# Chunked recurrence of an encoder block: order of the in-chunk products and place of the output products

## The chip, the cores and the metric

The kernel runs on one core of a Trainium2 chip. The metric is the device time of one execution in microseconds (us); lower is better. The engines are TensorE (PE, with its weight loads shown apart as PEld), VectorE (DVE), ScalarE (ACT), GpSimd (POOL) and SyncE (SP, which only issues transfers here).

## What is computed

One layer of a hybrid encoder on 256 tokens of width 2048, float32 in and out. The part that the change touches is the RWKV-7 time mixing: 16 heads of 64 features, scanned forward and backward. Cut to what matters:

```python
def wkv7_scan(r, w, k, v, kk, a, reverse):
    def step(state, inp):
        r_t, w_t, k_t, v_t, kk_t, a_t = inp
        sa = einsum('bhvk,bhk->bhv', state, kk_t)
        state = (state * w_t[:, :, None, :] - sa[..., None] * (kk_t * a_t)[:, :, None, :]
                 + v_t[..., None] * k_t[:, :, None, :])
        return state, einsum('bhvk,bhk->bhv', state, r_t)
    return lax.scan(step, zeros, xs, reverse=reverse)

o = head_group_norm(o_f + o_b, gn_g, gn_b)        # forward scan + backward scan
x = x + (sigmoid(gate_A) * (yA @ W_pA) + sigmoid(gate_B) * (yB @ W_pB)) @ W_out
x = x + ConvGLU(RMSNorm(x));  output = RMSNorm(x)
```

The large products around it (the input projection, the two branch projections, `W_out`, the three ConvGLU matrices) make up most of the arithmetic.

## The kernel before

All large products are one stream of weight chunks (`push`, `advance`, L191 to L249). A chunk is four blocks of 128x128 weights: SyncE loads it, ScalarE rounds it to a high part (L223), DVE makes the low part (L224), and PE runs per block one 512-wide matmul (L242, the high part against both parts of the activations) and one 256-wide matmul (L246, the low part). Splitting runs three chunks ahead of PE (`HL_AHEAD`).

The recurrence works on eight pairs of heads, the two heads of a pair on partitions 0 to 63 and 64 to 127 (index `hh`, "half"). A direction's 256 tokens are four chunks of 64 (`NC`, `C`). For each pair there are generators, which issue some instructions and then yield a pause: `rwkv_rates`, `rwkv_operands`, `rwkv_inverse`, `rwkv_chain`, `rwkv_norm`. `run` spreads a budget of weight chunks over these pauses, in proportion to their lengths, so that PE has weight-stream work while the other engines do the small steps. The loop over p sets the chain of pair p beside the inverse of pair p+1 (`abreast`: one step of each, then the inverse's pause), with the rates of pair p+2 at their side; then come the norm of pair p and the operands of pair p+2. The framework that compiles the program may still reorder instructions on an engine where it expects an operand to be late.

- `rwkv_inverse`: for each direction and each half, four products (L667), one per chunk, each with 64 rows by 128 columns, go into one PSUM bank of `ps_g` (two buffers); DVE multiplies the bank by a mask into `Gs` (L669). Then `keys_by_token` transposes keys through the same pool (L678), and six steps of 32x32 products (L704, L714, L725, twice) and two last ones (L744, L755) invert the triangles.
- `rwkv_chain`: for each of four steps i, products for Z (L783 or L786, 128x64 pieces of the array), a copy by ScalarE (L789), products for U (L795, 64x64 pieces), copies into `UV` (L799), products for the state S (L805, 128x64 pieces), and DVE's update of `ZR` (L814, L816). Pauses are `CY` long. After the four steps come the output products of all chunks: `UV` against `Gs` (L824, 128x64 pieces) and `ZR` against `AR` (L830, 64x64 pieces), which add up in one bank, chunks 0 and 1 ahead of a pause and 2 and 3 behind it. ScalarE copies the bank to `O` (L835). The chain has 13 pauses, the inverse 13.
- `rwkv_norm`: splits `O` (L173, L174) and sums over each head's features on PE (L540).

PSUM has eight banks: `ps_mm` 2, `ps_ms` 1, `ps_g` 2, `ps_t` 1, `ps_c` 2 (the chain's Z, U, S and outputs).

Of the kernel before, what the change touches and what calls it, by code (L numbers as in the profile page):

```python
# [17 lines left out]
P = 128  # L18
T = 256
# [12 lines left out]
# how the product stream is spread: weight chunks beside the gating unit, fill jobs beside each phase of the  # L32
# recurrence (LAST chunks stay for its end), and the weights of the phases' pauses
# [6 lines left out]
CHAIN_Y = 13 * CY  # L40
# [16 lines left out]
# per-feature vectors, one column per 128 features  # L57
# [12 lines left out]
# masks and identities, which depend on shapes alone  # L70
# [46 lines left out]
def hybrid_kernel(ctx: ExitStack, tc: tile.TileContext, xT, w_in, w_pa, w_pb, w_out, w_g, w_u, w_d,  # L117
# [24 lines left out]
    # derived columns  # L142
# [12 lines left out]
    # the first activation loads ACT's table beside the first loads  # L155
# [6 lines left out]
    def rsqrt(y, s, t):  # L162
        """y = s ** -0.5 elementwise (s, y, t: SBUF float32, distinct): a guess from the bits, two Newton steps."""
        V.tensor_scalar(out=y.bitcast(I32), in0=s.bitcast(I32), scalar1=-0.5, scalar2=RSQRT_MAGIC,
                        op0=ALU.mult, op1=ALU.add)
        for p1, p0 in ((-0.703952253, 0.703952253 * 2.38924456), (-0.5, 1.5 + 3.2e-7)):
            V.tensor_tensor(out=t, in0=y, in1=y, op=ALU.mult)
            V.scalar_tensor_tensor(out=t, in0=t, scalar=p1, in1=s, op0=ALU.mult, op1=ALU.mult)
            V.scalar_tensor_tensor(out=y, in0=t, scalar=p0, in1=y, op0=ALU.add, op1=ALU.mult)

    def split(dst, src):
        """dst[:, 0] + dst[:, 1] == src, each half exact in float32r."""
        A.copy(dst[:, 0], src)  # L173
        V.tensor_tensor(out=dst[:, 1], in0=src, in1=dst[:, 0].bitcast(F32), op=ALU.subtract)  # L174
# [10 lines left out]
    def push(wd, nk, act, done, wide=True):  # L185
        """queue one block of 128 features; done(PSUM tile): its halves sum to the product (wide: the high
        part of the weights passes once over [x_hi | x_lo]), or it is the product itself"""
        job = dict(wd=wd, nk=nk, act=act, done=done, wide=wide, ps=None, last=0)
        for k0 in range(0, nk, RK):
            n = min(RK, nk - k0)  # L190
            raws.append([job, k0, n, None])  # L191
            for s0 in range(0, n, HK):
                chunks.append([job, len(raws) - 1, s0, min(HK, n - s0), None])
        job["last"] = len(chunks)
        jobs.append(job)
        return job

    def pair_up(n):
        """the first two jobs of n raw loads each side by side: two products for each part of x that comes in"""
        order = [i + o for i in range(n) for o in (0, n)]  # L200
        at = {ri: i for i, ri in enumerate(order)}
        raws[:2 * n] = [raws[ri] for ri in order]
        first = sorted((c for c in chunks if c[1] < 2 * n), key=lambda c: at[c[1]])
        for i, c in enumerate(first):
            c[1] = at[c[1]]
            c[0]["last"] = i + 1
        chunks[:len(first)] = first
# [67 lines left out]
    # padded token buffers for the shift  # L275
# [5 lines left out]
    def feat(ft, outv, then=lambda: None):  # L281
        """token-shifted feature tile ft into outv ([P, T] or [P, 2, 128] view)."""
        return push(w_in[ft], KT, hact, lambda ps: shift(ft, ps, outv, then))
# [27 lines left out]
    def run(gens, budget, serial=False):  # L311
        """trace generators side by side (or one after the other), each (gen, sum of its pauses), with
        budget chunks of the product stream spread over their pauses"""
# [32 lines left out]
    # what waits for norm1 while the first products run  # L346
# [23 lines left out]
    # inner features of the decay and the rates, by direction: high and low parts, each on both partition halves  # L370
# [3 lines left out]
    # inner features of the gate: two parts of the first 128, and high, low, high parts of the last 32  # L374
# [79 lines left out]
    def abreast(*gens):  # L454
        """one step of each at a time; the pauses are those of the last"""
        live = list(gens)
        while live:
            step = 0
            for g in list(live):
                try:  # L460
                    step = next(g)
                except StopIteration:
                    live.remove(g)
            yield step
# [37 lines left out]
    # the mean's sum is done; u comes in beside the norm of v  # L502
# [9 lines left out]
    ps_c = es_r.enter_context(tc.tile_pool(name="ps_c", bufs=2, space=PSUM))  # L512
# [23 lines left out]
    def head_sums(b):  # L536
        """sums over each head's features"""
        ps = ps_ms.tile([P, 512], F32, name="ms", tag="ms")
        for o in range(2):
            PE.matmul(ps[:, 0:T], bones, b[:, o], start=(o == 0), stop=(o == 1))  # L540
        return ps[:, 0:T]


    def rwkv_rates(p):
        """decay and in-context rates, keys"""
        k, v3, r, _ = feats[p]
        # the matrices come on both partition halves; the upper half turns into the rounding errors of the lower
# [34 lines left out]
        # kk = normalised k * k_k  # L582
# [13 lines left out]
        # twice the direction's key  # L596
# [7 lines left out]
    def rwkv_operands(p):  # L604
        """the chunks' operands: decayed keys and queries, values by token"""
# [17 lines left out]
        # V with tokens on partitions, chunk pairs in both orders  # L623
# [6 lines left out]
        # [U | V] and [S | V] stacked on partitions, by step and direction  # L630
# [23 lines left out]
    def rwkv_inverse(p):  # L654
        """in-chunk products and the inverses of their triangles"""
# [3 lines left out]
        # in-chunk products: [beta | kappa]^T [alpha | rho | I]  # L659
        Gs = []  # L660
        for d in range(2):
            Gd = rt("Gs", [2, NC, 3, C], 4)
            for hh in range(2):
                rows = slice(C * hh, C * hh + C)
                gp = ps_g.tile([P, 512], F32, name="gp", tag="gp")
                for c in range(NC):
                    PE.matmul(gp[:, c * P:(c + 1) * P], BK[rows, d, c, hh:hh + 2, :].rearrange("p a b -> p (a b)"),  # L667
                              AR[rows, d, c].rearrange("p a b -> p (a b)"), start=True, stop=True)
                V.tensor_tensor(out=Gd[:, hh, :, 0:2, :].rearrange("p c a b -> p c (a b)"),  # L669
                                in0=gp.rearrange("p (c k) -> p c k", k=P),  # L670
                                in1=gmask[:, d, hh, None, :].to_broadcast([P, NC, P]), op=ALU.mult)
                yield GY
# [11 lines left out]
        # inverse of the unit triangular matrices I - A, A transposed being what Gs holds: exact on diagonal blocks of 2,  # L684
        # then of 8 and of 32. With Q the transposed inverse of the blocks so far and F = Q A' (A' the part of A^T that
        # the larger blocks add, F^4 = 0), the next Q is (I + F^2)(I + F) Q.
# [46 lines left out]
        # last doubling: the off-diagonal 32 x 32 block; Qf holds minus the transposed inverse  # L733
# [27 lines left out]
        # alpha in place of the used triangle: stacked operand of Z  # L761
# [8 lines left out]
    def rwkv_chain(p):  # L770
# [3 lines left out]
        # chunk recurrence, both directions side by side  # L774
        for i in range(NC):
# [21 lines left out]
            for hh in range(2):  # L797
                rows = slice(C * hh, C * hh + C)
                A.copy(UV[rows, i, :, hh, :], uc[rows, 0, :, 0:C])  # L799
            yield CY  # L800
            if i < NC - 1:
# [15 lines left out]
                yield CY  # L817
        # outputs of both directions
        oc = ps_c.tile([P, 512], F32, name="cc", tag="cc")
        for c in range(NC):  # L820
            st = (c, NC - 1 - c)
            for hh in range(2):
                for d in range(2):
                    PE.matmul(oc[C * hh:C * hh + C, C * c:C * c + C], UV[:, st[d], d, hh, :], Gs[d][:, hh, c, 1, :],  # L824
                              start=(d == 0), stop=False, tile_position=(0, C * hh))
            for d in range(2):
                for hh in range(2):
                    if st[d] > 0:
                        rows = slice(C * hh, C * hh + C)
                        PE.matmul(oc[rows, C * c:C * c + C], ZR[rows, st[d], d, hh, :], AR[rows, d, c, 1, :],  # L830
                                  start=False, stop=(d == 1 or st[1] == 0), tile_position=(C * hh, C * hh))
            if c == 1:
# [6 lines left out]
    def rwkv_norm(p):  # L839
        BK, UV, ZR, bv, lg = heads.pop(p)  # L840
        O = outs.pop(p)
        # head norm, gate
# [26 lines left out]
    # products that run beside the recurrence; what they give waits in DRAM  # L869
# [64 lines left out]
    # from here on there is room for loads that run further ahead  # L934
# [28 lines left out]
    # the rest of the stream; what its products read and feed is made below  # L963
# [111 lines left out]
def _lay_out(inp):  # L1075
# [6 lines left out]
    def feat_tiles(a):  # L1082
        """[..., 3488] -> [..., NFEAT * 128] in tile order"""
# [52 lines left out]
```

## Time and profile before

| | |
|---|---|
| time, median of 3 runs | 1585.49 us (1584.33, 1585.49, 1600.15) |
| span of the profiled execution, first to last instruction | 1582.7 us |
| PE busy | 1553.3 us, 98% |
| PE weight loads busy | 1349.3 us, 85% |
| DVE busy | 1223.6 us, 77% |
| ACT busy | 922.4 us, 58% |
| moved by DMA | 273.72 MB, mean 173 GB/s |
| granted TensorE clock, mean | 0.995 of full speed |

The profile lists the span of one execution; no other time of that execution is given. Matmuls are pipelined and the trace models their ends, so the distance from one start to the next says more than a duration, and a busy PE need not be a PE at its peak. Idle time of an engine that doesn't bound the stage costs nothing.

### The profile page before, as it was taken

How to read it: one execution, taken by the hardware profiler on the slowest of the kernel's cores; microseconds unless marked ns; L12 is line 12 of the kernel's file. 1: busy time of each engine (PE TensorE's matmuls, PEld its weight loads, DVE VectorE, ACT ScalarE, POOL GpSimd, SP SyncE). 2: the span in 40 equal slices, each digit the busy share in tenths (PEclk: the TensorE clock that was granted, in tenths of full speed). 3: DMA queues.
4: the chain of work that ended last, by engine and by line, in shares of the span. 5: the costliest groups of instructions: out<-in, count | busy, mean ns of one | idle time of the engine just before them, and what ended most of it. 6: DMA issues, size and time to landing. Idle time of an engine off the chain costs nothing.

```text
span 1582.7 us, 35532 instructions
## 1 busy us (share of the span) xinstructions
PE 1553.3 (98%) x13420; PEld 1349.3 (85%) x13420; DVE 1223.6 (77%) x2500; ACT 922.4 (58%) x1920; POOL 38.7 (2%) x65
## 2 busy tenths in 40 slices
PE   6999999999999999999999999999999999999996
PEld 5888888888888888799998888888888888888885
DVE  8888898888898887688668777777877776555554
ACT  5667765665666664455555666666665655545452
POOL 2000000000000000000000000000000000000000
PEclk9999999999999999999999999999999999999998
DMA  6555453443443433478555555555555556666663
GB/s 227 193 183 173 161 158 118 129 142 117 137 132 117 135 96 99 154 258 295 187 187 182 191 191 188 193 190 191 187 192 190 188 194 189 190 190 190 190 190 103
DMA packets 151501, 273.72 MB, mean 173 GB/s; under 512 B 16928, under 2 KB 23200, under 8 KB 151328
## 3 DMA queue, kind: packets, MB, share of 16 engines
q1 hardware_dynamic: 148624, 263.91, 52.7%
q0 software_dynamic: 2560, 7.34, 1.4%
q8 instruction: 105, 1.72, 0.4%
q14 instruction: 68, 0.56, 0.1%
q10 hardware_dynamic: 144, 0.19, 0.0%
HBM read 265.09 MB, written 6.29 MB: 171 GB/s over the span
## 4 chain that ended last, share of the span: by engine, by line
PE 84%; issue 9%; DVE 3%; DMA 2%; ACT 1%; POOL 0%; SPq 0%; DVEq 0%; ACTq 0%; POOLq 0%
PE mm L242 45%; PE mm L246 25%; PE mm L245 3%; PE mm L244 3%; PE gp L667 2%; DVE hl L224 1%; PE tp L714 1%; DMA raw<-in_w_in_dram 1%; PE tp L704 1%; PE tp L725 1%; PE ms L540 1%; PE cc L824 0%; ACT hl L223 0%; PE cc L795 0%; PE cc L830 0%
## 5 line engine op out<-in xcount | busy, mean ns | idle before, releaser
L242 PE MATMUL mm<-h,hl 128*128 128x512 f32 x2624 | 938.1, 400 | 8.1 <-DVE h L178 7.8
L224 DVE TENSOR_TENSOR hl<-raw,hl 128x512 fp32r<-128x512 f32 x960 | 655.6, 688 | 233.9 <-ACT hl L223 230.2
L223 ACT CAST hl<-raw 128x512 fp32r<-128x512 f32 x960 | 595.1, 622 | 402.7 <-PE mm L246 306.1
L246 PE MATMUL mm<-h,hl 128*128 128x256 f32 x2624 | 733.5, 280 | 4.3 <-DVE hl L224 4.3
L242 PEld LDWEIGHTS mm<-h,hl 128*128 128x128 f32 x2624 | 493.4, 188 | 124.0 <-ACT hl L223 8.1
L246 PEld LDWEIGHTS mm<-h,hl 128*128 128x128 f32 x2624 | 495.5, 189 | 6.9 <-DVE hl L224 6.2
L242 PE MATMUL mm<-act,hl 128*128 128x512 f32 x660 | 228.8, 394 | 0.0
L246 PE MATMUL mm<-act,hl 128*128 128x256 f32 x704 | 195.3, 277 | 0.0
L242 PEld LDWEIGHTS mm<-act,hl 128*128 128x128 f32 x660 | 123.8, 188 | 28.7
L258 ACT COPY ev<-mm 128x256 f32<-128x256 f32 x180 | 67.4, 374 | 118.4 <-PE mm L246 116.9
L246 PEld LDWEIGHTS mm<-act,hl 128*128 128x128 f32 x704 | 132.4, 188 | 0.0
L259 DVE TENSOR_TENSOR ev<-mm,ev 128x256 f32<-128x256 f32 x180 | 75.9, 422 | 57.9 <-ACT ev L258 56.5
L246 PE MATMUL mm<-mg,hl 128*128 128x256 f32 x256 | 71.9, 281 | 0.0
L244 PE MATMUL mm<-mg,hl 128*128 128x256 f32 x256 | 71.7, 280 | 0.0
L245 PE MATMUL mm<-mg,hl 128*128 128x256 f32 x256 | 71.2, 278 | 0.0
L244 PEld LDWEIGHTS mm<-mg,hl 128*128 128x128 f32 x256 | 48.1, 188 | 0.0
L245 PEld LDWEIGHTS mm<-mg,hl 128*128 128x128 f32 x256 | 48.1, 188 | 0.0
L246 PEld LDWEIGHTS mm<-mg,hl 128*128 128x128 f32 x256 | 48.1, 188 | 0.0
L242 PE MATMUL mm<-ya,hl 128*128 128x512 f32 x128 | 47.8, 405 | 0.0
L667 PE MATMUL gp<-AR,BK 64*128 64x128 f32 x256 | 39.8, 290 | 1.1 <-DVE BK L618 1.1
L1033 ACT ACTIVATE gt<-cp,colt 128x256 f32<-128x256 f32 x44 | 26.5, 603 | 19.2 <-DVE cp L1031 19.2
L667 PEld LDWEIGHTS gp<-AR,BK 64*128 64x128 f32 x256 | 31.4, 187 | 6.1 <-DVE BK L618 1.5
(285 smaller groups left out, 1556.0 us busy)
## 6 DMA issues: line engine op xcount, KB each, us to landing
raw<-in_w_in_dram SPq DMA_DIRECT2D x304, 256.0 KB, 3.0
raw<-in_w_g_dram SPq DMA_DIRECT2D x176, 256.0 KB, 3.1
raw<-in_w_u_dram SPq DMA_DIRECT2D x176, 256.0 KB, 3.0
raw<-in_w_d_dram SPq DMA_DIRECT2D x176, 256.0 KB, 3.0
raw<-in_w_out_dram SPq DMA_DIRECT2D x64, 256.0 KB, 3.0
raw<-in_w_pa_dram SPq DMA_DIRECT2D x32, 256.0 KB, 2.9
raw<-in_w_pb_dram SPq DMA_DIRECT2D x32, 256.0 KB, 4.7
spill<-ev POOLq DMA_DIRECT2D x32, 128.0 KB, 3.1
```

Source lines behind the costliest of these rows:

```text
L223: A.copy(hl[:, 0, :m], raw[:, s0:s0 + m])
L224: V.tensor_tensor(out=hl[:, 1, :m], in0=raw[:, s0:s0 + m], in1=hl[:, 0, :m].bitcast(F32), op=ALU.subtract)
L242: PE.matmul(ps[:, 0:512], hl[:, 0, j], a.rearrange("p a t -> p (a t)"), start=(k == 0), stop=False)
L244: PE.matmul(ps[:, 0:256], hl[:, 0, j], a[:, 0], start=(k == 0), stop=False)
L245: PE.matmul(ps[:, 0:256], hl[:, 0, j], a[:, 1], start=False, stop=False)
L246: PE.matmul(ps[:, 0:256], hl[:, 1, j], a[:, 0], start=False, stop=(k == job["nk"] - 1))
L258: A.copy(t, ps[:, 256:512])
L259: V.tensor_tensor(out=t, in0=ps[:, 0:256], in1=t, op=ALU.add)
L540: PE.matmul(ps[:, 0:T], bones, b[:, o], start=(o == 0), stop=(o == 1))
L667: PE.matmul(gp[:, c * P:(c + 1) * P], BK[rows, d, c, hh:hh + 2, :].rearrange("p a b -> p (a b)"), AR[rows, d, c].rearrange("p a b -> p (a ...
L704: PE.matmul(xv[qs, d, c], Gs[d][qs, q // 2, c, 0, b0:b0 + 32], Tc[qs, d, c], start=True, stop=True, tile_position=(32 * q, 32 * q))
L1033: A.activation(gt, b[:, 1:T + 1], AF.Identity, scale=col("cw1", f), bias=col("cb", f))
```

## The change

In `rwkv_inverse` both halves of a direction get their PSUM bank at once, and the products go chunk by chunk, half 0 and half 1 in turn; the two masks follow, and then one pause of twice the length. The inverse has two pauses fewer. In `rwkv_chain` the output products move into the steps: `ZR` against `AR` (for i > 0) right behind the products for U, and `UV` against `Gs` at the end of the step, behind the products for S; they add up over the whole chain in a bank of their own, `ps_o`, and `ps_c` keeps one buffer. The pauses in the chain become 12, and `CHAIN_Y` with them. The diff also takes comments away; these hunks are left out.

```diff
-CHAIN_Y = 13 * CY
+CHAIN_Y = 12 * CY
...
-    ps_c = es_r.enter_context(tc.tile_pool(name="ps_c", bufs=2, space=PSUM))
+    ps_c = es_r.enter_context(tc.tile_pool(name="ps_c", bufs=1, space=PSUM))
+    ps_o = es_r.enter_context(tc.tile_pool(name="ps_o", bufs=1, space=PSUM))
...
         for d in range(2):
             Gd = rt("Gs", [2, NC, 3, C], 4)
+            gps = [ps_g.tile([P, 512], F32, name="gp", tag="gp") for _ in range(2)]
+            for c in range(NC):
+                for hh in range(2):
+                    rows = slice(C * hh, C * hh + C)
+                    PE.matmul(gps[hh][:, c * P:(c + 1) * P], BK[rows, d, c, hh:hh + 2, :].rearrange("p a b -> p (a b)"),
+                              AR[rows, d, c].rearrange("p a b -> p (a b)"), start=True, stop=True)
             for hh in range(2):
-                rows = slice(C * hh, C * hh + C)
-                gp = ps_g.tile([P, 512], F32, name="gp", tag="gp")
-                for c in range(NC):
-                    PE.matmul(gp[:, c * P:(c + 1) * P], BK[rows, d, c, hh:hh + 2, :].rearrange("p a b -> p (a b)"),
-                              AR[rows, d, c].rearrange("p a b -> p (a b)"), start=True, stop=True)
                 V.tensor_tensor(out=Gd[:, hh, :, 0:2, :].rearrange("p c a b -> p c (a b)"),
-                                in0=gp.rearrange("p (c k) -> p c k", k=P),
+                                in0=gps[hh].rearrange("p (c k) -> p c k", k=P),
                                 in1=gmask[:, d, hh, None, :].to_broadcast([P, NC, P]), op=ALU.mult)
-                yield GY
+            yield 2 * GY
             Gs.append(Gd)
...
+        oc = ps_o.tile([P, 512], F32, name="oc", tag="oc")
         for i in range(NC):
...
                 A.copy(UV[rows, i, :, hh, :], uc[rows, 0, :, 0:C])
+
+            for d in range(2 if i > 0 else 0):
+                for hh in range(2):
+                    rows = slice(C * hh, C * hh + C)
+                    PE.matmul(oc[rows, C * cs[d]:C * cs[d] + C], ZR[rows, i, d, hh, :], AR[rows, d, cs[d], 1, :],
+                              start=False, stop=False, tile_position=(C * hh, C * hh), skip_group_check=True)
             yield CY
...
                     V.tensor_tensor(out=ZR[rows, i + 1, :, hh, :], in0=src, in1=PC[rows], op=ALU.mult)
-                yield CY
-        # outputs of both directions
-        oc = ps_c.tile([P, 512], F32, name="cc", tag="cc")
-        for c in range(NC):
-            st = (c, NC - 1 - c)
-            for hh in range(2):
-                for d in range(2):
-                    PE.matmul(oc[C * hh:C * hh + C, C * c:C * c + C], UV[:, st[d], d, hh, :], Gs[d][:, hh, c, 1, :],
-                              start=(d == 0), stop=False, tile_position=(0, C * hh))
+
             for d in range(2):
                 for hh in range(2):
-                    if st[d] > 0:
-                        rows = slice(C * hh, C * hh + C)
-                        PE.matmul(oc[rows, C * c:C * c + C], ZR[rows, st[d], d, hh, :], AR[rows, d, c, 1, :],
-                                  start=False, stop=(d == 1 or st[1] == 0), tile_position=(C * hh, C * hh))
-            if c == 1:
+                    PE.matmul(oc[C * hh:C * hh + C, C * cs[d]:C * cs[d] + C], UV[:, i, d, hh, :],
+                              Gs[d][:, hh, cs[d], 1, :], start=(i == 0 and d == 0), stop=(i == NC - 1 and d == 1),
+                              tile_position=(0, C * hh), skip_group_check=True)
+            if i < NC - 1:
                 yield CY
         O = rt("O", [T])
         A.copy(O, oc[:, 0:T])
```

## Rows read from the trace of the kernel before

**Rows 1.** Windows: length; busy us of PE, PEld, DVE, ACT, POOL; clock, DMA.

```profile
180.00:680.00 500.00, 499.10 (x6962) 411.56 (x6963) 420.58 (x965) 296.72 (x719) 23.29 (x43) 1.00 0.41 129
```

**Rows 2.** Waits of PE, 180 to 680 us: total, times, longest.

```profile
PE gp L667 <- DVE BK L618: 1.1, 1, 1.1
```

**Rows 3.** Timeline of PE: start, duration, line, tile, count; one round.

```profile
241.88 0.40 PE L242 MATMUL mm<-h,hl 128*128 128x512 f32 x1
242.11 0.28 PE L246 MATMUL mm<-h,hl 128*128 128x256 f32 x1
242.32 0.45 PE L805 MATMUL cc<-UV,Gs 128*64 128x64 f32 x8
242.70 1.16 PE L667 MATMUL gp<-AR,BK 64*128 64x128 f32 x8
243.79 0.50 PE L242 MATMUL mm<-h,hl 128*128 128x512 f32 x1
244.12 0.28 PE L246 MATMUL mm<-h,hl 128*128 128x256 f32 x1
244.24 0.40 PE L242 MATMUL mm<-h,hl 128*128 128x512 f32 x1
```

**Rows 4.** Timeline of PE at 182 us: a group of products that was split.

```profile
182.45 0.48 PE L667 MATMUL gp<-AR,BK 64*128 64x128 f32 x2
182.86 0.49 PE L242 MATMUL mm<-h,hl 128*128 128x512 f32 x1
```

**Rows 5.** Timeline of PE at 598 us: two groups of products run into each other.

```profile
597.73 1.26 PE L667 MATMUL gp<-AR,BK 64*128 64x128 f32 x12
598.92 0.33 PE L786 MATMUL cc<-ZR,Gs 128*64 128x64 f32 x2
599.18 0.71 PE L667 MATMUL gp<-AR,BK 64*128 64x128 f32 x4
```

**Rows 6.** Timeline of weight loads: a stretch of 8, and that at 598 us.

```profile
549.86 0.96 PEld L667 LDWEIGHTS gp<-AR,BK 64*128 64x128 f32 x8
...
597.73 1.07 PEld L667 LDWEIGHTS gp<-AR,BK 64*128 64x128 f32 x12
```

**Rows 7.** Timeline of PE, outputs of a pair's first two chunks.

```profile
281.80 0.46 PE L824 MATMUL cc<-Gs,UV 128*64 128x64 f32 x8
282.19 0.33 PE L830 MATMUL cc<-AR,ZR 64*64 64x64 f32 x4
282.45 0.46 PE L824 MATMUL cc<-Gs,UV 128*64 128x64 f32 x8
282.83 0.45 PE L830 MATMUL cc<-AR,ZR 64*64 64x64 f32 x8
283.21 0.45 PE L744 MATMUL tp<-Tc,Gs 32*32 32x32 f32 x32
```

**Rows 8.** Groups by line: count | busy us, mean ns | idle before, releaser.

```profile
L667 PE MATMUL gp<-AR,BK 64*128 64x128 f32 x256 | 39.8, 290 | 1.1 <-DVE BK L618 1.1
...
L824 PE MATMUL cc<-Gs,UV 128*64 128x64 f32 x256 | 14.7, 234 | 0.0
...
L830 PE MATMUL cc<-AR,ZR 64*64 64x64 f32 x192 | 12.5, 234 | 0.0
```

**Rows 9.** Windows of one pair: in-chunk products, inverse steps, end and norm.

```profile
297.10:311.50 14.40, 14.40 (x109) 11.80 (x108) 12.44 (x28) 5.78 (x15) 0.54 (x1) 1.00 0.44 139
311.50:345.00 33.50, 33.50 (x608) 28.09 (x606) 31.58 (x77) 20.41 (x48) 1.08 (x2) 1.00 0.40 125
345.00:359.50 14.50, 14.47 (x171) 11.69 (x166) 9.97 (x23) 11.85 (x32) 1.08 (x2) 1.00 0.43 141
```

**Rows 10.** Groups by line on DVE: the masks of the in-chunk products.

```profile
L669 DVE TENSOR_TENSOR Gs<-gp,cst 128x512 f32<-128x512 f32 x32 | 22.0, 688 | 7.3 <-PE gp L667 6.9
```

**Rows 11.** Timelines of ACT and PE: the outputs' copy, then the norm's sums.

```profile
287.11 0.37 ACT L835 COPY O<-cc 128x256 f32<-128x256 f32 x1
...
289.94 0.40 PE L540 MATMUL ms<-bs,bones 128*128 128x256 f32 x2
```

## What was predicted

> **What bounds the kernel now.** I read the views in this order. First the page's busy times, where TensorE (PE) leads; that alone says little, as ends of matmuls are modelled. Then the windows by stage: the change touches only the recurrence, which runs from about 180 to 680 us; there PE is busy 499.1 of 500 us, VectorE (DVE) 420.6, ScalarE 296.7 [rows 1]. Then PE's waits in that stretch: the longest is a single one of 1.1 us, on the first pair's operands [rows 2]. So in this stage no other engine ends last; a microsecond that PE is spared is a microsecond of the end, until DVE, at 84%, has no slack left. The DMA queues carry nothing that the change touches.
>
> Then PE's timeline, which shows what its time is made of. The reader is to look at the differences of the starts, not at the durations. In the plain stream a 512-wide matmul is followed after 0.23 us and a 256-wide one after 0.12 us; a chunk is four of each, 1.40 us. Around a group that uses part of the array (64 rows, or 64 columns) the same starts stretch: 0.21 for 0.12 ahead of it, 0.33 for 0.23 behind it [rows 3]. Every change between the full array, 128x64, 64x128, 64x64 and 32x32 pieces costs something by itself.
>
> **Prices from these rows.** A float32 matmul is two instructions in the trace. An in-chunk product (L667, 64 rows by 128 columns): a stretch of 8 instructions takes 1.09 us [rows 3], one of 2 takes 0.41 [rows 4], so one costs (1.09 - 0.41) / 6 = 0.113 us, and a stretch 0.18 above that. An output product (64 wide): 8 take 0.38 and 4 take 0.26, so one costs 0.03 us [rows 7]. A change of the piece of the array: in rows 3 there are three (full, 128x64, 64x128, full) and what is over is 0.09 + (0.38 - 8 x 0.03) + (1.09 - 8 x 0.113) + 0.10 = 0.52 us, or 0.17 each; in rows 7 the outputs' cluster takes 283.21 - 281.80 = 1.41 us for 28 instructions, 0.57 above 28 x 0.03, with four changes, or 0.14 each. I take 0.16, with 0.14 and 0.17 as bounds.
>
> **Part one: alternating halves.** 256 instructions [rows 8] run in the order c0 half 0, c0 half 1, c1 half 0 and so on, where all four chunks of one half came first. Nothing is added; each direction now fills two PSUM banks before DVE reads either. Do two halves run at once? Before has no such order on purpose, but once the order that was scheduled ran two groups into each other: 12 instructions take 598.92 - 597.73 = 1.19 us, where 12 in a row would take 12 x 0.113 + 0.18 = 1.54; three steps of 0.113 are missing [rows 5]. The 12 and the 4 that follow at 599.18 are two groups of eight, so at most four could overlap, and about three did. The weight loads did so too: 12 take 1.07 us, 8 take 0.96 [rows 6]. The Trainium skill ("TensorE: Matmul & The Clock Gate", section "LDWEIGHTS (loading the stationary operand)") prices a load by its columns alone, 128 / 1.2 GHz = 107 ns whatever its rows; were the loads of both halves to queue, 256 of them would still ask for 27.3 us (an estimate from that page) and this part would bring nothing. By that rule the sum would be the first rival's; the rows speak against it, as four loads more cost 0.11 us and not 0.43.
> In a stretch of 16 that alternates, with the first and the last alone, 16 go in 9 steps: 7 steps saved in each of 16 stretches, 112 x 0.113 = 12.7 us. Bounds: every one overlapped, 128 x 0.113 = 14.5; only one in four, as in rows 5 (3 of 12), 64 x 0.113 = 7.2. I take 12.7, since in rows 5 the overlap was near all that the order allowed.
>
> **Part two: fewer changes of the piece.** Chain of pair p and inverse of pair p+1 go round by round, one step of each and then weight chunks. I count the changes that each round's steps force, from the code. Before, 13 rounds: rounds 1 to 4 (chain step, then 64x128 products) 3 each, round 5 (chain, transposes on the full array) 2, rounds 6 to 11 (chain, 32x32 steps) 3 each, rounds 12 and 13 (the outputs' 128x64, 64x64, 128x64, 64x64 and then 32x32, as in rows 7) 6 each: 12 + 2 + 18 + 12 = 44. After, 12 rounds: the 64x64 output products stand right behind the 64x64 products of U, and the 128x64 ones right behind the 128x64 products of S, without a change of their own. Rounds 1 and 2 have 3, round 3 has 2, rounds 4 to 11 have 3, round 12 (the last outputs alone) 2: 6 + 2 + 24 + 2 = 34. That is 10 less in each of 7 rounds of pairs, 4 less in the first inverse, which runs alone (24 to 20), 8 less in the last chain (32 to 24): 82 in all, 82 x 0.16 = 13.1 us (11.5 to 13.9). The output products themselves (32 and 24 instructions per pair, [rows 8]) are moved, not removed, at the same 0.03.
>
> **What the moves can cost.** The one PSUM buffer of the chain instead of two: each step's product already needs what ScalarE or DVE read out of the step before, so no wait is new; nothing, and the outputs' own bank is read out before the next pair's chain begins. Two waits are new or less covered.
> First, the second direction's products, and the transposes behind them, need both banks back, so both masks (L669, 0.688 us each [rows 10]) stand between, 1.4 us, behind whatever DVE has queued. Between them lies the same pause as before, 3 units, two chunks or 2.8 us. So it is covered where DVE is abreast; in these rounds DVE is busy 12.44 of 14.40 us [rows 9], and PE will now want them in some 2 us less. Nothing, or one pair of masks for each of the 8 inverses, 11 us. Queued behind a waiting product on PE would be the whole weight stream. I take 0.2 per pair.
> Second, the outputs' way to the head norm: the copy of O starts at 287.11 and the sums that need it at 289.94 [rows 11], 2.8 us, which two chunks cover. After, the pauses' budget is used up before the last step, and the norm starts right behind it, with one chunk of cover at first: nothing where later chunks are scheduled between (PE's order does mix: a chunk's first matmul stands between two parts of one group of products [rows 4]), else one chunk, 1.4 us a pair, 11 us. I take 0.3 per pair.
> DVE gets no less work: in one pair's rounds it has 12.44 + 31.58 + 9.97 = 53.99 us of 62.4 [rows 9]; PE's 62.4 less 3.2 leaves 59.2, so DVE stands at 91%. It does not become the bound on average; only in the middle stretch, 31.58 of 33.50, is there little slack, and that stretch loses no PE time. Three chunks split ahead (4.2 us of PE) carry DVE over the dense rounds.
> Sum: 12.7 + 13.1 - 8 x 0.5 = 21.8 us off PE, and off the end. The profiled span of 1582.7 us becomes 1560.9. The median of the runs, 1585.49, is 2.8 us above that span, which I keep: 1563.7, say 1563 us.
>
> **Rivals.** (a) The halves don't run at once, because their loads or products share a path: then the alternation is worth nothing, and 13.1 - 4 = 9 us are left, 1576. For it: load and product of one half go at the same 0.113 us. Against it: rows 5 and 6. (b) The time goes into the waits, since PE catches DVE up: both waits at their bounds cost 22 of the 25.8 us, 1582; at half of that 15 us are left, 1571; I write 1576 between them. For it: DVE at 86 and 94% in two of the three stretches of a pair. Against it: the 1.1 us of waits of a PE that runs beside it today, and three chunks split ahead. (c) Slower: the second direction's products stand at the head of PE until DVE has masked both banks, and splits queued ahead of these masks starve the stream behind. It decides from 25.8 / 8 = 3.2 us a pair on; slower by over 1% takes 5.2 us a pair, a whole chunk's cover and more lost in each direction: about 1605. Nothing in before waits so long. (d) More than forecast: all overlap, price 0.17, and fewer groups split by the schedule: 14.5 + 13.9 + 3, with no waits, 1554.
>
> **Numbers.** Forecast 0.66 (its own range 1556 to 1570), (a) 0.10, (b) 0.15, (c) 0.05, (d) 0.04. The range for 8 in 10 goes from (d)'s edge into (a) and (b): 1554 to 1579. A change of this kernel's time under about 1%, 16 us, could hardly be told from none. Below 1569.6: nearly all of the forecast, (d), and a tenth of (a) and (b), 0.70; over 1601.3: 0.04; the rest, 0.26, within 1%.
>
> **What the profile after would show.** Part one: 16 in-chunk instructions in about 1.2 us, starts in pairs, and their line's busy time near 20 us instead of 39.8. Part two: no output stretch between two 32x32 groups, output products directly behind U's and S's, clusters of 1.41 us gone. The stage's end moves from about 680 to 658, with PE idle there below 6 us; after it nothing changes. I am wrong if PE waits on the masks, on O or on split weights for over 10 us in the stage, if the 16 instructions take over 1.9 us, or if the changes cost PE less than 0.1 us each once the groups stand together.

## The result, and the profile after

The changed kernel takes 1569.49 us (median of 11 runs, 1567.25 to 1583.23), the one before 1585.42 us (11 runs beside them): a ratio of 0.9886, 95% interval 0.9858 to 0.9913, so 1.1% faster. The forecast was 1563 in a range of 1554 to 1579: direction and range hold, the gain is smaller, about 16 us where 22 were forecast. The profiled execution spans 1565.5 us, 17.2 less than before. Executions of these kernels, the one before among them, fall into two groups some 12 to 15 us apart, and the traces place that difference behind the recurrence, so below kernels are compared within one group, or by the length of the recurrence alone.

The recurrence's window after, with the columns of [rows 1]:

```profile
180.00:680.00 500.00, 493.68 (x7056) 409.96 (x7056) 433.70 (x998) 306.36 (x743) 23.96 (x45) 1.00 0.44 140
```

The same 500 us hold more of the program (7056 PE instructions, 6962 before), and PE is idle in them for 6.3 us instead of 0.9. Its longest waits from 170 to 680 us (engine, line, releaser: total, times, longest; the first products now start at 179.1), where [rows 2] had one of 1.1 us:

```profile
PE tp L707 <- DVE Tc L699: 2.9, 5, 0.8
PE gp L669 <- DVE BK L619: 0.9, 1, 0.9
PE mm L242 <- ACT hl L223: 0.6, 1, 0.6
PE mm L246 <- DVE hl L224: 0.6, 1, 0.6
PE tp L707 <- DVE Tc L733: 0.6, 3, 0.2
```

The longest is new: the first 32x32 step of the inverse (L707, L704 before) waits for DVE's transpose (L699). No wait on the masks (L672) is there.

The in-chunk products in PE's timeline, for [rows 3], [rows 4] and [rows 5]:

```profile
232.07 0.45 PE L788 MATMUL cc<-ZR,Gs 64*64 64x64 f32 x8
232.44 1.16 PE L669 MATMUL gp<-AR,BK 64*128 64x128 f32 x16
233.54 0.50 PE L242 MATMUL mm<-h,hl 128*128 128x512 f32 x1
```

Sixteen instructions take 1.10 us from start to start, as long as eight took before (1.09): eight steps of 0.113 and the 0.18 that a stretch costs above them. In such a whole stretch all of the overlap is there. The outputs, for [rows 7]:

```profile
243.86 0.45 PE L816 MATMUL cc<-UV,Gs 128*64 128x64 f32 x8
244.14 0.40 PE L831 MATMUL oc<-Gs,UV 128*64 128x64 f32 x8
244.48 1.09 PE L681 MATMUL gp<-cst,BK 128*128 128x128 f32 x8
...
251.44 0.45 PE L800 MATMUL cc<-Z,Qf 64*64 64x64 f32 x8
251.72 0.40 PE L809 MATMUL oc<-AR,ZR 64*64 64x64 f32 x8
252.05 1.10 PE L717 MATMUL tp<-FQ,K 32*32 32x64 f32 x64
```

S's products now take 0.28 us up to the outputs behind them, where they took 0.38 up to a change of the piece [rows 3]. But at the head of five of the eight pairs the order on PE looks like this:

```profile
350.10 0.44 PE L788 MATMUL cc<-ZR,Gs 64*64 64x64 f32 x6
350.47 0.38 PE L541 MATMUL ms<-bs,bones 128*128 128x256 f32 x1
350.78 0.32 PE L788 MATMUL cc<-ZR,Gs 64*64 64x64 f32 x2
351.04 0.49 PE L669 MATMUL gp<-AR,BK 64*128 64x128 f32 x4
351.46 0.39 PE L541 MATMUL ms<-bs,bones 128*128 128x256 f32 x1
351.77 0.93 PE L669 MATMUL gp<-AR,BK 64*128 64x128 f32 x10
352.64 0.38 PE L541 MATMUL ms<-bs,bones 128*128 128x256 f32 x1
352.95 0.49 PE L669 MATMUL gp<-AR,BK 64*128 64x128 f32 x2
```

The sums over features (L541), late on the other engines, are scheduled into the middle of the next pair's products; the first two here belong to the norm, the third to `rwkv_operands`. Each takes 0.31 us there, with a change of the array to full and one back, where in the plain stream two of them take 0.25. In groups of lines, for [rows 8]:

```profile
L669 PE MATMUL gp<-AR,BK 64*128 64x128 f32 x256 | 25.6, 293 | 0.9 <-DVE BK L619 0.9
...
L831 PE MATMUL oc<-Gs,UV 128*64 128x64 f32 x256 | 13.6, 225 | 0.3 <-ACT UV L804 0.3
...
L809 PE MATMUL oc<-AR,ZR 64*64 64x64 f32 x192 | 9.6, 219 | 0.0
```

And one pair's windows for [rows 9] (products, inverse, end and norm):

```profile
291.00:304.20 13.20, 13.20 (x96) 10.41 (x94) 11.77 (x27) 6.39 (x16) 0.54 (x1) 1.00 0.37 114
304.20:338.10 33.90, 33.08 (x619) 28.12 (x618) 31.27 (x77) 19.43 (x45) 0.54 (x1) 1.00 0.36 121
338.10:350.00 11.90, 11.90 (x152) 9.84 (x150) 9.84 (x21) 10.47 (x30) 1.62 (x3) 1.00 0.59 181
```

A pair takes 59.0 us where it took 62.4. DVE has 52.9 of them, 90%, where it had 87%.

**Where PE's time went.** Adding up the distances from each start to the next over all of PE's timeline, by what the instruction does, with the idle time ahead of an instruction taken out into a row of its own (us):

| | before | after | difference |
|---|---|---|---|
| in-chunk products | 36.7 | 23.4 | -13.2 |
| products for U | 12.1 | 9.9 | -2.2 |
| products for S | 9.3 | 6.8 | -2.5 |
| outputs, `ZR` against `AR` | 10.2 | 7.9 | -2.4 |
| outputs, `UV` against `Gs` | 12.4 | 11.3 | -1.1 |
| the weight stream | 1373.8 | 1371.4 | -2.4 |
| products for Z (split by sums) | 13.9 | 14.6 | +0.7 |
| sums over features | 9.8 | 11.7 | +1.9 |
| all else | 74.7 | 73.8 | -0.9 |
| PE idle | 7.4 | 12.4 | +5.0 |

The changes of the array's piece, counted in the same timelines, went from 401 to 328. The stretches of in-chunk products went from 44 to 31: nine of the 16 directions are split by other instructions, and one that is not (at 538.92 us) took 1.64 us where the other six took 1.09 or 1.10.

### The profile page after: what moved, and what is told of

Its sections match the earlier page's. It is cut to its first block, busy times and chain, and to the rows that moved or that the text cites. A ratio compares the mean times of both kernels' runs of the same rounds, so it can differ in the third digit from the quotient of the medians.

```text
span 1565.5 us, 35582 instructions
## 1 busy us (share of the span) xinstructions
PE 1531.2 (98%) x13420; PEld 1333.2 (85%) x13420; DVE 1222.2 (78%) x2500; ACT 922.6 (59%) x1920; POOL 37.9 (2%) x65
## 4 chain that ended last, share of the span: by engine, by line
PE 84%; issue 9%; DVE 4%; DMA 1%; ACT 1%; POOL 0%; SPq 0%; DVEq 0%; ACTq 0%; POOLq 0%
PE mm L242 45%; PE mm L246 26%; PE mm L244 3%; PE mm L245 3%; PE gp L669 1%; PE tp L717 1%; PE ms L541 1%; DVE hl L224 1%; DVE FQ L695 1%; PE tp L707 1%; PE cc L800 0%; DMA xt<-in_xT_dram 0%; PE tp L728 0%; DMA spill<-ev 0%; POOL spill L877 0%
## 5 line engine op out<-in xcount | busy, mean ns | idle before, releaser
L224 DVE TENSOR_TENSOR hl<-raw,hl 128x512 fp32r<-128x512 f32 x960 | 655.9, 689 | 231.0 <-ACT hl L223 227.3
L246 PE MATMUL mm<-ybs,hl 128*128 128x256 f32 x128 | 36.2, 283 | 0.0
L245 PE MATMUL mm<-ybs,hl 128*128 128x256 f32 x128 | 36.2, 283 | 0.0
```

Of the source, the lines that this page charges most:

```text
L224: V.tensor_tensor(out=hl[:, 1, :m], in0=raw[:, s0:s0 + m], in1=hl[:, 0, :m].bitcast(F32), op=ALU.subtract)
L245: PE.matmul(ps[:, 0:256], hl[:, 0, j], a[:, 1], start=False, stop=False)
L246: PE.matmul(ps[:, 0:256], hl[:, 1, j], a[:, 0], start=False, stop=(k == job["nk"] - 1))
```

## The experiments

All traces are compared by the recurrence: from the start of the first in-chunk product to the start of the last stretch of small products. Four of these stretches hold 16 more matmuls of the weight stream than the others (before, e1, e6, e7); 16 x 0.175 = 2.8 us is taken off them (0.175 is the mean step of the stream, [rows 3]). "Time" is the difference of the medians to before. Each recurrence is that of one execution: two traces of one kernel differ by 1.1 us (changed, a0) and by 0.1 (e8, twice), so a difference of about a microsecond says nothing by itself.

| kernel | recurrence, us | to before | changes | products' steps, us | time to before, us |
|---|---|---|---|---|---|
| before | 488.3 | | 401 | 36.7 | |
| changed | 471.4 | -16.9 | 328 | 23.4 | -16 |
| a0: changed, again | 472.5 | -15.8 | 328 | 23.4 | -15 |
| e1: halves alone | 475.4 | -12.9 | 388 | 22.7 | -13 |
| e2: outputs alone | 480.0 | -8.3 | 336 | 35.9 | -7 |
| e3: half after half | 475.8 | -12.5 | 328 | 28.8 | -12 |
| e4: outputs between | 477.9 | -10.4 | 361 | 21.4 | -10 |
| e5: pause behind keys | 469.5 | -18.8 | 326 | 23.9 | -19 |
| e6: pause first | 475.8 | -12.5 | 307 | 20.1 | -13 |
| e7: both pauses | 469.1 | -19.2 | 303 | 20.8 | -20 |
| e8: two pauses | 466.3 | -22.0 | 323 | 21.1 | -22 |
| e9: copies early | 470.6 | -17.7 | 327 | 22.4 | -18 |
| e10: two pauses, copies early | 470.7 | -17.6 | 332 | 23.4 | -18 |

> The changed kernel once more, beside the three kernels of this call on the same chip: recurrence about 471 us from its first to its last small product, 15 to 18 us faster than before.

It came as expected.

**e1, one part alone.** In the kernel before:

```diff
-            for hh in range(2):
-                rows = slice(C * hh, C * hh + C)
-                gp = ps_g.tile([P, 512], F32, name="gp", tag="gp")
-                for c in range(NC):
+            gps = [ps_g.tile([P, 512], F32, name="gp", tag="gp") for _ in range(2)]
+            for c in range(NC):
+                for hh in range(2):
+                    rows = slice(C * hh, C * hh + C)
...
+            for hh in range(2):
...
-                yield GY
+            yield GY
+            yield GY
```

> The kernel before with the alternating halves alone; outputs, chain and the number of pauses stay as before (two pauses after each direction's products). My theory (the halves overlap fully, as 16 products in 1.09 us show in the trace after): 128 steps x 0.113 = 14.5 us less, and two stretches of products fewer per pair, about 2 x 8 x 0.16 = 2.6 us, minus waits of 1 to 2 us: 13 to 17 us faster than before, products' line near 25 us busy. Rival (the halves share a path and the gain comes from fewer changes of the piece alone): 2 to 4 us faster.

12.9 us less in the recurrence, as much in the time; the products' steps fall by 14.0 us. This is just under the theory's lower edge, and the rival is out: with only 13 changes fewer it could not be that much. Hardly anything waits: besides the first pair's 1.1 us PE has 0.6 us of waits on the transpose and 0.6 on the sums.

**e2, the other part alone.** The changed kernel with before's products and their four pauses.

> The changed kernel with the in-chunk products as before, half after half with a pause behind each; outputs in the chain's steps. Counted from the code 37 changes of the piece per pair instead of 44, and 8 fewer in the last chain: 57 x 0.16 = 9 us. My theory: 6 to 9 us faster than before, PE's output clusters gone. Rival (the moved outputs bring nothing, since their cover of the norm's sums is lost): within 3 us of before.

8.3 us less (7 in the time), as expected, with 65 changes fewer. So the two parts alone make 12.9 + 8.3 = 21.2 us, and the two together 16.9: 4.3 us are lost where they meet.

**e3, no alternation.** In the changed kernel:

```diff
-            for c in range(NC):
-                for hh in range(2):
+            for hh in range(2):
+                for c in range(NC):
```

> The changed kernel with one edit: the 16 product instructions of a direction run half 0 first and half 1 then, into the same two banks, with the same masks and pauses. My theory (overlap of the halves): 16 go in about 1.9 to 2.0 us instead of 1.09, so 13 to 14 us slower than the changed kernel. Rival (fewer changes and fewer pauses did it): within 2 us of the changed kernel.

4.4 us slower than the changed kernel (3.3 than a0), not 13 to 14: a miss. The whole stretch shows why:

```profile
233.80 1.71 PE L669 MATMUL gp<-AR,BK 64*128 64x128 f32 x16
235.44 0.50 PE L242 MATMUL mm<-h,hl 128*128 128x512 f32 x1
```

Sixteen take 1.64 us, 13 steps of 0.113 and 0.18: three steps overlap at the seam between the halves, the three that [rows 5] had shown. So a stretch of 16 gains 0.54 us by alternating, not 0.9. And most groups are split by the schedule: a part of 10 that spans the seam takes 0.88 us here and 0.86 in the changed kernel. Over all stretches the products' steps are 28.8 against 23.4 us. The overlap is real, but more than half of part one's gain (36.7 to 28.8 of 36.7 to 23.4) comes from putting both halves side by side at all: 13 stretches fewer, at 0.18 us above their steps, are 2.3 us of it, and the overlap at the seam is the rest.

**e4, more changes of the piece.** In the changed kernel the loop over `ZR` against `AR` moves from behind U's copies to directly ahead of the `UV` against `Gs` products.

> The changed kernel with the 64x64 output products moved from behind U's products to behind S's, between these and the 128x64 output products. Work and waits stay; changes of the array's piece grow by two in steps 1 and 2 and by one in step 3, 5 per pair, 40 in all. My theory (a change costs 0.14 to 0.17 us): 5.5 to 7 us slower than the changed kernel. Rival (a change costs nothing by itself, and the clusters' time before was their work): within 2 us.

6.5 us slower in the recurrence (5.4 than a0), with 33 changes more (not 40, as the sums now stand alone among small pieces 5 times instead of 13): 0.16 to 0.20 each, some of it waits, as PE is idle in the recurrence for 7.3 us against 5.1 (6.1 in a0). Its second step in PE's timeline:

```profile
259.68 0.45 PE L811 MATMUL cc<-UV,Gs 128*64 128x64 f32 x8
260.06 0.45 PE L827 MATMUL oc<-AR,ZR 64*64 64x64 f32 x8
260.44 0.45 PE L831 MATMUL oc<-Gs,UV 128*64 128x64 f32 x8
260.82 0.75 PE L728 MATMUL tp<-K,K 32*32 32x32 f32 x64
```

Each eight take 0.38, where 0.28 and 0.34 stand in the changed kernel. The rival, that a change costs nothing by itself, is out.

**e5, a pause moved.** The sum of the pauses stays, and `KY` is 1.6:

```diff
-            yield 2 * GY
+            yield (4 * GY - KY) / 2
...
         keys_by_token(1)
-        yield 1.2
+        yield 1.2 + KY
```

> The changed kernel with its pauses shifted: 2.2 instead of 3.0 behind each direction's products, 2.8 instead of 1.2 behind the transposed keys; the sum is the same. My theory (the first 32x32 step now comes before DVE has made its operand, since masks, predicated copies and transpose follow both directions' products at once): PE's waits on that transpose fall from 2.9 us to under 1, the Z products ahead of it lose their 2.5 us, and the kernel is 2 to 3 us faster than the changed one. Rival (that wait only shows where PE would have waited anyway, as DVE is the bound there): the wait moves to the masks or the weight splits, and the time stays within 1 us.

3.0 us less than a0 in the recurrence, 3.6 in the time, a little above the expectation. PE's waits:

```profile
PE gp L670 <- DVE BK L620: 1.1, 1, 1.1
PE tp L708 <- DVE Tc L700: 0.9, 4, 0.2
PE tp L708 <- DVE Tc L734: 0.8, 3, 0.4
```

**e6, a pause ahead of the first step.** `yield BEGIN_Y` (2.5) opens both generators, and both sums of pauses grow by it.

> The changed kernel with a pause of 2.5 ahead of the first step of chain and inverse, so that weight chunks stand between the norm and the first products. My theory (the norm's sums, late on DVE, are now taken in the middle of the products, and each takes two changes of the piece of the array): 307 changes instead of 328 and 20 stretches of products instead of 31, 21 x 0.16 to 0.20 = 3.4 to 4.2 us, plus what the sums and the split chain products lost by themselves, about 1: 3.5 to 5.5 us faster than the changed kernel. Rival (the splits fill time in which PE would wait): within 1 us.

A miss: 3.3 us slower than a0. The mechanism did what was said (307 changes, products' steps 20.1 us, no sums among them), but PE now waits:

```profile
PE tp L709 <- DVE Tc L701: 6.1, 5, 1.9
PE ms L542 <- ACT bs L174: 3.0, 7, 1.0
PE gp L671 <- DVE BK L620: 1.1, 1, 1.1
```

The wait on the transpose doubled (2.9 in the changed kernel), and 3.0 us on the sums came in.

**e7, both.**

> Both shifts of pauses together. My theory, two separate losses: 6 to 8 us faster than the changed kernel, about 1562 where the changed one takes 1569. Rival (one and the same DVE backlog stands behind both): no more than the better of the two alone.

3.4 us less than a0, 0.4 less than e5 alone. Not two separate losses: the rival's figure holds. With the transpose in time, the first pause takes 3.1 us off the products' steps, but PE then waits 3.6 us on the sums.

**e8, two pauses again.** One edit to the changed kernel:

```diff
-            yield 2 * GY
+            yield GY
+            yield GY
```

> The changed kernel with its one pause of twice the length behind each direction's products cut into two, so that the inverse has 13 pauses again beside the chain's 12 and both parts of the change are otherwise there. My theory (the new waits come from the two missing rounds: products, keys and the first 32x32 step follow one another with fewer chain steps and chunks between; neither the halves alone nor the outputs alone had them, and both had 13 rounds): no waits on the transpose, the norm's sums stand alone between small products 6 times instead of 13, and the two parts add up, 12.9 + 8.3 = 21 us faster than before in the recurrence, 4 to 5 faster than the changed kernel. Rival (DVE is the bound once PE has less to do, as the pause put first suggests): the waits turn up elsewhere, within 1.5 us of the changed kernel.

As the theory had it: 22.0 us less than before, against 21.2 for the two parts added up, and 5 to 6 us less than the changed kernel.

```profile
PE gp L669 <- DVE BK L619: 1.1, 1, 1.1
PE ms L630 <- DVE O L849: 0.9, 3, 0.4
PE mm L242 <- ACT hl L223: 0.8, 1, 0.8
PE mm L246 <- DVE hl L224: 0.6, 1, 0.6
```

The wait on L699's transpose (L700 here) is gone, and the sums stand alone between small pieces 6 times instead of 13. The pair that is shown for the changed kernel further down, here:

```profile
300.90 1.16 PE L669 MATMUL gp<-AR,BK 64*128 64x128 f32 x16
...
309.39 0.44 DVE L700 STREAM_TRANSPOSE Tc<-FQ 128x256 f32<-128x256 f32 x1
...
310.66 0.75 PE L708 MATMUL tp<-Tc,Gs 32*32 32x32 f32 x64
```

DVE's transpose is done 8.9 us after the second direction's products start, and PE comes to its first 32x32 step after 9.8.

> The kernel with two pauses once more, in more rounds, as the one that beats both: recurrence 466 to 467 us, 20 to 22 us faster than before.

466.4 us, the same, and in time again 21 us less than before.

**e9 and e10, DVE's copies earlier.** In the changed kernel, and in e8, the 64 predicated copies that stood behind both directions' products follow each direction's masks.

> The changed kernel with DVE's predicated copies of a direction right behind that direction's masks, instead of all 64 behind both directions: 4 x 0.3 = 1.2 us of DVE work per pair leaves the stretch between the second products and the first 32x32 step. My theory: PE's waits on that transpose fall from 3 us to under 1, the kernel is 2 to 3.5 us faster than the changed one, as with the pause moved there (3.6). Rival (DVE's backlog, not the order, sets the wait): within 1 us.

> Two pauses and early copies together. My theory: no more than the two pauses alone give, within 1.5 us of them, since there the transpose is no longer waited for. Rival: another 2 to 3 us on top.

e9 gains 0.8 to 1.9 us, less than expected: the wait on L699's transpose is gone, but others take its place.

```profile
PE cc L790 <- DVE ZR L826: 1.3, 3, 0.5
PE gp L669 <- DVE BK L619: 0.9, 1, 0.9
PE gp L568 <- DVE lw L560: 0.9, 1, 0.9
```

e10 is 4.4 us slower than e8. Both expectations for it missed: the transpose was in time already, PE's waits on DVE's low parts (L224) rise from 0.6 to 1.5 us, and in the order that was scheduled 9 more changes of the piece and 2.3 us more of products' steps come with it. That the early copies delay DVE's low parts is likely, but not shown.

## Why the prediction was right, and where it was off

**What bounds the stage.** Right: PE set the end, and what PE was spared came off it. The limit named beside it, DVE's slack, was nearer than the sum took it: the share came out as forecast (90% in a pair, 91 forecast), but in e6 and e9 the gain went into waits, most of them on DVE, and what brought more (e5, e7, e8) gave DVE more time ahead of its transpose.

**Part one.** 12.7 us forecast, 13.2 measured, but that the two agree is in part luck. 2.3 of the 13.2 are the 13 stretches fewer at 0.18 us, which the prediction had booked under the changes of part two (an estimate). The overlap itself gave 10.9 us, some 97 steps where 112 were forecast: a whole stretch takes eight steps where nine were forecast, but nine of the 16 directions are split, and one took 1.64 us, with its starts spaced as in e3. So the line's busy time is 25.6 us and not near 20. Rival (a), that the loads would queue and leave 16 steps, falls: 16 took eight. The reason given for it was too simple: e3 shows that a good part needs no alternation.

**Part two.** 82 changes fewer at 0.16, or 13.1 us, were forecast; 73 fewer came. The sums, which the schedule set alone among small pieces 13 times instead of 5, add 16; elsewhere seven more went than the count had. The count was made from the code's order, though [rows 4] already showed that the schedule mixes. In time the lines of U, S, both outputs and the stream give 2.2 + 2.5 + 2.4 + 1.1 + 2.4 = 10.6 us, and the 2.3 us of the products' stretches belong here too. The price of a change was right: without PE's idle time the recurrence got 21.4 us shorter, 10.9 of it overlap, and 10.5 / 73 = 0.14; reckoned the same way e2 gives 0.15 and e4, against the changed kernel, 0.17, the forecast's bounds being 0.14 and 0.17.

**Waits.** The step that was off most. 4.0 us forecast; idle time, sums and the split Z products took 5.0 + 1.9 + 0.7 = 7.6, and at another place. The masks' wait, put at 0.2 a pair, did not show. The way to the sums was late, as forecast for the norm, but cost changes of the piece rather than idle PE. The step left out: behind the masks DVE has eight predicated copies a pair and a transpose before the first 32x32 step can start, and with the pauses merged PE gets from the second direction's products to that step over two chain steps, where it has three in e8. In the trace after, DVE from the second direction's masks on:

```profile
301.09 1.29 DVE L672 TENSOR_TENSOR Gs<-gp,cst 128x512 f32<-128x512 f32 x2 [0.75 <-PE gp L669]
...
306.91 1.86 DVE L695 COPY_PREDICATED FQ<-cst,Gs 32x128 f32<-32x128 int32 x6
308.80 0.69 DVE L224 TENSOR_TENSOR hl<-raw,hl 128x512 fp32r<-128x512 f32 x1
309.41 0.44 DVE L699 STREAM_TRANSPOSE Tc<-FQ 128x256 f32<-128x256 f32 x1
```

The second direction's products had started at 300.10; DVE's transpose is done 9.8 us later. PE's Z products started at 308.63, so PE was there after 8.9 us, and its L707 started only at 309.90. That the merged pause did it is shown, not argued: e1 and e2, each with 13 rounds, hardly wait there; e3, with the merged pause and slower products, waits as long as the changed kernel (2.6 us); cutting the pause in two (e8) takes the wait away and makes the two parts add up. The change's third edit, one pause of twice the length, which the prediction took for "the same pause as before", so cost 5 us. Not all of it is idle time: e8 also has fewer split stretches (26 for 31) and fewer sums that stand alone.

**The sum.** In spans 12.7 + 13.1 - 4.0 = 21.8 became 13.2 + 10.6 - 7.6 = 16.2, and 0.9 from all other lines makes 17.1 of the 17.2. The last 1.3 us between the two medians is the profiled execution, the fastest of the eleven: the typical gap of median and span after is 4.0 us, where 2.8 was carried over. Rival (b), DVE's backlog eating part of the gain, is thus true for about a quarter of it (5.0 us of idle time of 21.8); (c) and (d) did not happen. e8, 5 to 6 us below the changed kernel, comes to about the forecast's 1563.

## What to carry to other kernels

Products that fill half the array's rows belong side by side, and small products of one shape behind one another: a change of the piece cost 0.14 to 0.17 us each time here, where a whole stretch of eight small products takes 0.28 to 0.38. Count these changes in the order that the engine really gets, not in the source. When steps are merged to please one engine, look up what the next engine must do between them: a pause that seems empty for PE may be the time that DVE lives on.

## What the runs showed that was not expected

Products on the other half of the rows run beside the first half's without any alternation, but only near the seam: three of 16 steps overlap (1.64 us against 1.10 when alternated). And a PE that loses its small extra work does not always get faster: in e6 21 changes fewer and 3.3 us less of product steps came with 6.1 us of waits on the transpose and 3.0 on the sums.
